# The q and k columns of each attention head as one Strassen pair among the pairs of u and gates

## The chip, the core and the metric

The kernel runs on one core of a Trainium2 chip. The core has five engines with queues of their own: TensorE (PE, matrix products), VectorE (DVE), ScalarE (ACT), GpSimd (POOL) and SyncE (SP, which here only issues transfers). Each works through its queue in order; engines wait for each other by semaphores. On chip are SBUF, from which all engines read, and PSUM, eight banks into which PE writes its sums. The metric is the device time of one execution in microseconds, lower is better; the median of several runs counts.

## What is computed

One layer over 512 tokens of 2048 channels, in float32:

```
h = rms_norm(x)
q | k | v | u | v_sgu | gate_a | gate_b = h @ w_in      # 1024 x5 and 2048 x2 columns
q = rms_norm per head (8 heads of 128) * g_q;  k the same * g_k
z = q k^T / sqrt(128);  beta = sigmoid(z);  keep = sigmoid(-z), s < t only
A[t,s] = beta[t,s] * product of keep[t,j] over s < j < t
y_a = (A v) @ w_oa
y_b = (gelu(u) * (W_s layer_norm(gelu(v_sgu)) + b)) @ w_ob
x = x + (sigmoid(gate_a) * y_a + sigmoid(gate_b) * y_b) @ w_out
x = x + relu(rms_norm(x) @ w_ff1)^2 @ w_ff2               # hidden 8192
```

## The kernel before

Every operand of a large product is held as two parts in a faster matmul format (`hi`, a rounded copy made by ACT, and `lo`, the rest, made by DVE), and a product is three matmuls: hi·hi, hi·lo, lo·hi (`mm3`, lines 70 to 74). A weight piece of 128x1024 is loaded raw, cast by ACT (line 94 or 108) and subtracted by DVE (line 96 or 109) into the pool of pieces `w_piece`, six buffers, so three hi/lo pairs.

Two ways of multiplying stand side by side. `by_token` takes 512 weight columns at a time, holds four PSUM banks (one per 128 tokens) and runs over all 16 row blocks: 192 matmuls of 512 columns. `strassen_pair` takes two blocks of 128 columns and the two halves of the tokens, forms Strassen's seven products (`strassen_columns`, lines 200 to 236; the weight sums on DVE in `Sums.parts`, one of them by an accumulating load that POOL issues, line 183) and leaves the result with channels on the partitions and tokens along the row. Products of one pair and the copies between banks use two of the five banks of `ps_acc`; the three of `ps_aux` hold the forks for the whole run of pairs.

The order of the program around the change: q and k by `by_token` (`heads_of`), v, all twice (four heads each), then v_sgu by `by_token`, then a run of 20 pairs for u and the gates, then y_a and y_b. Beside these products stands a queue of small tasks, `behind`: `step()` takes one from it after each weight piece of `by_token` and after each product of a pair. Through it go the loading of x, the transposes of q and k to channels (`head`), the attention of four heads at once (`attention`: weights, turn, product), the spatial weights and the Strassen factors of h (`gate_factors`, needed before the run of pairs). The final order on each engine is made by a scheduler when the program is built, which starts from the order written and takes what it holds ready first.

For q and k, `heads_of` scales the rows, sums squares per head on POOL and DVE, multiplies by the reciprocal root, and transposes each head's four blocks on PE (line 526). In `weights`, z is `mm3` for each of four token blocks (512, 384, 256, 128 columns), two sigmoids on ACT give beta and keep, DVE does the mask, a running product from the right (line 554) and the multiplication (line 558); `turn` transposes A (line 568) and splits it; `product` multiplies with v and POOL stores the result to memory (`held_o`).

Of the kernel before, what the change touches and what calls it, by code (L numbers as in the profile page):

```python
# [35 lines left out]
def tile_hybrid_layer(ctx: ExitStack, tc: tile.TileContext, x, g_mix, w_in, g_q, g_k, ln_g, ln_b,  # L36
# [426 lines left out]

    load_xk(0)
# [5 lines left out]
    for k in range(CK):  # L470
# [3 lines left out]
    early.extend([weight(w_in[0], CK, 0), (hi, lo)])  # L474
# [3 lines left out]
                   lambda: turn_gains(gains, gT2),  # L478
                   lambda: along(rstd, rstd_b)])
# [7 lines left out]
    scale = float(P) ** -0.5  # L487
# [13 lines left out]
    def heads_of(c0, g0, half, name):  # L501

        n, parts = [], []

        def evac(tb, o):
            raw = slot(name + "_raw")
            nc.scalar.activation(out=raw, in_=o, func=AF.Copy, scale=rstd[:, tb:tb + 1])
            sq = slot("sq")
            nc.gpsimd.tensor_tensor(out=sq, in0=raw, in1=raw, op=ALU.mult)
            m = tiny(4, "m")  # L510
            nc.vector.tensor_reduce(out=m, in_=sq.rearrange("p (h d) -> p h d", d=P), axis=AX.X,
                                    op=ALU.add)
            nc.vector.tensor_scalar(out=m, in0=m, scalar1=1.0 / P, scalar2=EPS, op0=ALU.mult,
                                    op1=ALU.add)
            r = rsqrt(m, 4, "r")
            raw3 = raw.rearrange("p (h d) -> p h d", d=P)
            nc.vector.tensor_tensor(out=raw3, in0=raw3, in1=r.unsqueeze(2).to_broadcast([P, 4, P]),
                                    op=ALU.mult)
            n.append(raw)

        by_token(win, c0 + half * W, hT_at, KT, evac, name)

        def head(h):
            t = aux(name + "T")
            for tb in range(NTB):
                nc.tensor.transpose(out=t[:, tb * P:(tb + 1) * P], in_=n[tb][:, h * P:(h + 1) * P],
                                    identity=ident)
# [6 lines left out]
    def attention(half, qT, kT, v):

        a, aT = {}, {}

        def weights(h):

            room = {0: ("a", 384), 1: ("b", 0), 2: ("a", 0), 3: ("c", 0)}  # L540
            beta = {k: slot("beta") for k in "abc"}
            for tb in (3, 2, 1, 0):
                n = (tb + 1) * P
                key, c = room[tb]
                z = aux("z")
                mm3(z[:, :n], [q[:, tb * P:n] for q in qT[h]], [k[:, :n] for k in kT[h]], True, True)
                b = beta[key][:, c:c + n]
                keep = slot("keep")
                nc.scalar.activation(out=keep[:, :n], in_=z[:, :n], func=AF.Sigmoid, scale=-scale)
                nc.scalar.activation(out=b, in_=z[:, :n], func=AF.Sigmoid, scale=scale)  # L550
                nc.vector.tensor_tensor(out=keep[:, n - P:n], in0=keep[:, n - P:n], in1=later, op=ALU.max)

                rest = slot("rest")
                nc.vector.tensor_tensor_scan(out=rest[:, :n][:, ::-1], data0=keep[:, :n][:, ::-1],
                                             data1=keep[:, :n][:, ::-1], initial=1.0,
                                             op0=ALU.mult, op1=ALU.min)
                nc.gpsimd.tensor_tensor(out=b[:, n - P:], in0=b[:, n - P:], in1=past, op=ALU.mult)
                nc.vector.tensor_tensor(out=b[:, :n - 1], in0=b[:, :n - 1], in1=rest[:, 1:n], op=ALU.mult)
                a[h, tb] = b

        def turn(h):

            hi = {k: slot("aT_hi", F32R) for k in "abc"}
            lo = {k: slot("aT_lo", F32R) for k in "abc"}
            for sb in range(NTB):
                t = aux("aT")
                for tb in range(sb, NTB):
                    nc.tensor.transpose(out=t[:, tb * P:(tb + 1) * P],
                                        in_=a[h, tb][:, sb * P:(sb + 1) * P], identity=ident)
                key, c = {0: ("a", 0), 1: ("b", 0), 2: ("c", 0), 3: ("b", 384)}[sb]  # L570
                n = S - sb * P
                parts = hi[key][:, c:c + n], lo[key][:, c:c + n]
                split_to(*parts, t[:, sb * P:])
                aT[h, sb] = parts

        def product(h):
            o = aux("o")
            for sb in range(NTB):
                mm3(o[:, sb * P:], [p[:, h * P:(h + 1) * P] for p in v[sb]], aT[h, sb],
                    sb == 0, sb == NTB - 1)  # L580
            for i, part in enumerate(split(o, "oT")):
                nc.gpsimd.dma_start(out=held_o[half * 4 + h, i], in_=f32(part))
# [72 lines left out]

# [402 lines left out]
```

## Time and profile before

| | |
|---|---|
| median of three runs | 2428.63 us (2428.33 to 2431.28) |
| profiled execution, its own time | 2426.78 us |
| its span, first to last instruction | 2425.1 us |
| granted PE clock | 1.00 |
| PE, DVE, ACT, POOL busy | 100%, 76%, 49%, 17% |
| q, k, v, v_sgu with attention | 8 to 419 us |
| 20 pairs of u and gates | 419 to 809 us |
| DMA busy share in the pairs | 0.68 |

In the views, a group's row gives the line, engine and operation, output<-inputs, sizes and count, then busy time in all and the mean duration of one, then idle time before it and who ended it. PE's instructions overlap, so that the distance between two starts and not the duration is what one costs. In a timeline row the first number is the start in us, the second the time covered.

### The profile page before, as it was taken

The numbers are of one execution on the slowest core, as the hardware profiler recorded it, in microseconds if no ns is written. First come the engines' busy times: TensorE is split into PE (matmuls) and PEld (weight loads), VectorE is DVE, ScalarE is ACT, GpSimd is POOL, SyncE is SP. The second block draws the span as 40 slices with busy tenths as digits, with TensorE's granted clock in tenths as the row PEclk, the third lists the DMA queues.
The fourth block names the chain that finished last, engine by engine and source line by source line (L and its number), as shares of the span: only waits on it lengthen the run. The fifth ranks groups of instructions, "written<-read, shape, count | busy, mean of one in ns | idle before, by whom it ended". The sixth has DMA issues, their size and how long they took to land.

```text
span 2425.1 us, 34336 instructions
## 1 busy us (share of the span) xinstructions
PE 2414.5 (100%) x12648; PEld 2073.7 (86%) x12648; DVE 1848.1 (76%) x2433; ACT 1199.5 (49%) x1769; POOL 410.3 (17%) x539
## 2 busy tenths in 40 slices
PE   9999999999999999999999999999999999999999
PEld 8888878888888888888988888899888888888887
DVE  4556578777777564444789888888888998989987
ACT  5233344555555322233577776777765443333333
POOL 0203112000011422100001000000024334322210
PEclk9999999999999999999999999999999999999999
DMA  5333234666666944343389888888886999867753
GB/s 183 95 123 104 96 101 151 154 163 165 163 157 159 345 140 148 131 148 124 102 219 238 225 227 233 232 233 223 224 276 247 298 309 320 255 218 209 235 181 97
DMA packets 446169, 463.68 MB, mean 191 GB/s; under 512 B 19568, under 2 KB 330928, under 8 KB 446000
## 3 DMA queue, kind: packets, MB, share of 16 engines
q1 hardware_dynamic: 358352, 332.48, 42.5%
q0 software_dynamic: 87360, 128.48, 23.1%
q8 instruction: 99, 1.62, 0.3%
q10 hardware_dynamic: 288, 0.52, 0.1%
q14 instruction: 70, 0.57, 0.1%
HBM read 374.90 MB, written 85.46 MB: 190 GB/s over the span
## 4 chain that ended last, share of the span: by engine, by line
PE 63%; DVE 0%; ACT 0%; issue 0%; DVEq 0%
PE q L73 9%; PE q L72 9%; PE q L74 9%; PE q L220 7%; PE fork L220 7%; PE fork L223 4%; PE q L223 4%; PE xo L74 2%; PE xo L72 2%; PE xo L73 2%; PE yb L73 1%; PE yb L72 1%; PE yb L74 1%; PE f L73 0%; PE f L74 0%; PE f L72 0%
## 5 line engine op out<-in xcount | busy, mean ns | idle before, releaser
L108 ACT CAST w_hi<-w_raw 128x1024 fp32r<-128x1024 f32 (+1 forms) x583 | 611.9, 1050 | 656.9 <-PE q L73 334.6
L109 DVE TENSOR_TENSOR w_lo<-w_raw,w_hi 128x1024 fp32r<-128x1024 f32 (+1 forms) x583 | 710.7, 1220 | 202.0 <-ACT w_hi L108 192.4
L73 PE MATMUL q<-w_lo,ys 128*128 128x512 f32 x896 | 348.9, 389 | 0.3 <-DVE w_lo L109 0.3
L74 PE MATMUL q<-w_hi,ys 128*128 128x512 f32 x896 | 348.6, 389 | 0.0
L72 PE MATMUL q<-w_hi,ys 128*128 128x512 f32 x896 | 312.6, 389 | 0.7 <-ACT w_hi L108 0.5
L96 DVE TENSOR_TENSOR w_lo<-w_raw,w_hi 128x1024 fp32r<-128x1024 f32 x131 | 164.5, 1255 | 194.1 <-ACT w_hi L94 193.1
L94 ACT CAST w_hi<-w_raw 128x1024 fp32r<-128x1024 f32 x131 | 137.5, 1050 | 316.1 <-issue 81.3
L220 PE MATMUL q<-ys,w_hi 128*128 128x512 f32 x1064 | 271.5, 393 | 0.0
L183 POOL DMA_DIRECT2D w_raw<-in_w_ff_dram x58 | 81.1, 1398 | 900.8 <-ACT act L281 463.1
L220 PE MATMUL fork<-ys,w_hi 128*128 128x512 f32 x904 | 225.9, 391 | 0.0
L220 PEld LDWEIGHTS q<-ys,w_hi 128*128 128x128 f32 x1064 | 189.7, 189 | 31.9
L73 PEld LDWEIGHTS q<-w_lo,ys 128*128 128x128 f32 x896 | 168.2, 188 | 36.4 <-DVE w_lo L109 1.5
L72 PEld LDWEIGHTS q<-w_hi,ys 128*128 128x128 f32 x896 | 168.1, 188 | 36.3 <-ACT w_hi L108 0.9
L74 PEld LDWEIGHTS q<-w_hi,ys 128*128 128x128 f32 x896 | 168.2, 188 | 34.8
L220 PEld LDWEIGHTS fork<-ys,w_hi 128*128 128x128 f32 x904 | 164.5, 189 | 30.8
L957 POOL DMA_DIRECT2D ys<-store x224 | 127.6, 614 | 177.7 <-PE q L74 115.9
L223 PEld LDWEIGHTS q<-ys,w_lo 128*128 128x128 f32 x1064 | 144.8, 190 | 10.6
L223 PE MATMUL q<-ys,w_lo 128*128 128x256 f32 x1064 | 148.0, 282 | 0.0
L1000 DVE SCALAR_TENSOR_TENSOR total<-q,plus,total 128x512 f32<-128x512 f32 x180 | 132.1, 746 | 4.6 <-PE q L74 4.5
L223 PEld LDWEIGHTS fork<-ys,w_lo 128*128 128x128 f32 x904 | 123.3, 190 | 8.8
L223 PE MATMUL fork<-ys,w_lo 128*128 128x256 f32 x904 | 126.1, 282 | 0.0
L74 PE MATMUL q<-ys,w_lo 128*128 128x256 f32 x408 | 115.5, 283 | 0.0
(283 smaller groups left out, 4596.2 us busy)
## 6 DMA issues: line engine op xcount, KB each, us to landing
w_raw<-in_w_ff_dram SPq DMA_DIRECT2D x256, 512.0 KB, 5.6
w_raw<-in_w_in_dram SPq DMA_DIRECT2D x143, 512.0 KB, 4.0
ys<-store POOLq DMA_DIRECT2D x224, 256.0 KB, 6.3
w_raw<-in_w_ff_dram POOLq DMA_DIRECT2D x58, 512.0 KB, 7.3
store<-ys_hi SPq DMA_DIRECT2D x90, 256.0 KB, 4.6
store<-ys_lo SPq DMA_DIRECT2D x90, 256.0 KB, 5.3
w_raw<-in_w_out_dram SPq DMA_DIRECT2D x32, 512.0 KB, 4.2
store<-ys SPq DMA_DIRECT2D x44, 256.0 KB, 5.7
```

Source lines behind the costliest of these rows:

```text
L72: nc.tensor.matmul(o, lhsT=lh[0], rhs=rh[0], start=start, stop=False, **kw)
L73: nc.tensor.matmul(o, lhsT=lh[0], rhs=rh[1], start=False, stop=False, **kw)
L74: nc.tensor.matmul(o, lhsT=lh[1], rhs=rh[0], start=False, stop=stop, **kw)
L94: nc.scalar.copy(out=hi, in_=raw)
L96: nc.vector.tensor_tensor(out=lo, in0=raw, in1=f32(hi), op=ALU.subtract)
L108: nc.scalar.copy(out=hi, in_=src)
L109: state["lo"] = nc.vector.tensor_tensor(out=lo, in0=src, in1=f32(hi), op=ALU.subtract)
L183: state["sum"] = nc.gpsimd.dma_start(out=self.w21, in_=self.blocks[1, 1], accum_op=ALU.add)
L220: nc.tensor.matmul(o, lhsT=hi[:, k, :], rhs=rhs[name][k], start=name == "y11" and k == 0, stop=False, skip_group_check=True)
L223: nc.tensor.matmul(o[:, :HS], lhsT=lo[:, k, :], rhs=rhs[name][k][:, :HS], start=False, stop=k == KH - 1, skip_group_check=True)
L957: nc.gpsimd.dma_start(out=f32(t), in_=store[f][HELD.index(name), p])
L1000: nc.vector.scalar_tensor_tensor(out=a, in0=o, scalar=part, in1=a, op0=ALU.mult, op1=ALU.add)
```

## The change

The 1024 columns of q and of k leave `by_token`. For each head, the 128 columns of q and the 128 of k become the two column blocks of one `strassen_pair`, in the run of u and gates: two gate pairs, then eight times (one head's pair, two gate pairs), then two gate pairs, 28 in all. The result of such a pair is already q and k with channels on the partitions, so that the transposes fall away. What each token's row still needs is its norm: `attend` squares the pair's result on ACT, splits it, sums over the channels with matmuls against a tile of ones (`factors`, four columns wide, output `ms`), and takes the reciprocal root on POOL. The factor of q enters z as the scale of the sigmoids; the factor of k goes along the row by a matmul of ones with diagonal tiles (`scaled_k`, output `rows`) and is multiplied into k with the gains. Attention of one head is 18 tasks, one per product of the pairs after its own. v is now stored in memory by POOL (`held_a`) and fetched for each head; `held_o` is stored by SP in place of POOL. The attention's PSUM tiles come from `ps_acc`, the pool of the products. The factors of h and the spatial weights are made during v and v_sgu.

The diff, cut to its core:

```diff
     def column_sums(wap, c0, loaded=True):
 
         KH = KT // 2
-        blocks = {(h, c): wap[:, c0 + c * P:c0 + (c + 1) * P].rearrange("(k h p) c -> h p k c", p=P, h=2)[h]
+        c0 = c0 if isinstance(c0, tuple) else (c0, c0 + P)
+        blocks = {(h, c): wap[:, c0[c]:c0[c] + P].rearrange("(k h p) c -> h p k c", p=P, h=2)[h]
                   for h in range(2) for c in range(2)}
...
+    gqk = const.tile([P, HEADS], F32, name="gqk")
+    eps_x = const.tile([P, NTB], F32, name="eps_x")
+
+    def head_terms():
+        nc.vector.tensor_tensor(out=gqk, in0=gT2[:, 16:24], in1=gT2[:, 24:32], op=ALU.mult)
+        nc.vector.tensor_scalar(out=gqk, in0=gqk, scalar1=-float(P) ** 0.5, scalar2=0.0, op0=ALU.mult, op1=ALU.add)
+        nc.vector.tensor_scalar(out=eps_x, in0=ms1, scalar1=P * EPS, scalar2=0.0, op0=ALU.mult, op1=ALU.add)
...
+    held_a = dram.tile([2, 2, NTB, P, W], F32, name="held_a")
...
-    def heads_of(c0, g0, half, name):
...
+    def attend(h, act):
+
...
+        def square(src):
+            t = slot("sq")
+            nc.scalar.activation(out=t, in_=src, func=AF.Square)
+            part["sq"] = split(t, "sq")
+
+        def factors():
+            m = acc("ms")
+            for tb in range(NTB):
+                for i, sq in enumerate(part["sq"]):
+                    nc.tensor.matmul(m[:, tb * 4:tb * 4 + 4], lhsT=sq[:, tb * P:(tb + 1) * P], rhs=ones_r[:, :4],
+                                     start=i == 0, stop=i == 1)
+            t, f = small4("ms"), small4("r")
+            nc.vector.tensor_tensor(out=t, in0=m[:, :16].rearrange("p (b r) -> p b r", r=4)[:, :, 0], in1=eps_x,
                                     op=ALU.add)
+            nc.gpsimd.tensor_tensor(out=f, in0=t, in1=mhalf, op=ALU.pow)
+            return f
+
+        def of_q():
+            r[1], r[-1] = factors(), small4("nr")
+            nc.gpsimd.tensor_tensor(out=r[-1], in0=r[1], in1=minus_one, op=ALU.mult)
+            part["q"] = split(q, "qT")
+
+        def of_k():
+            f, f_hi, f_lo = factors(), small4("r_hi", F32R), small4("r_lo")
+            nc.vector.tensor_copy(out=f_hi, in_=f)
+            nc.vector.tensor_tensor(out=f_lo, in0=f, in1=f32(f_hi), op=ALU.subtract)
+            part["dg"] = [slot("dg", F32R) for _ in range(2)]
+            for t, x in zip(part["dg"], (f32(f_hi), f_lo)):
+                for tb in range(NTB):
+                    nc.scalar.activation(out=t[:, tb * P:(tb + 1) * P], in_=ident, func=AF.Copy,
+                                         scale=x[:, tb:tb + 1])
+
+        def scaled_k():
+            rows = acc("rows")
+            for i, t in enumerate(part["dg"]):
+                nc.tensor.matmul(rows, lhsT=ones_r, rhs=t, start=i == 0, stop=i == 1)
+            nc.vector.scalar_tensor_tensor(out=k, in0=k, scalar=gqk[:, h:h + 1], in1=rows, op0=ALU.mult,
+                                           op1=ALU.mult)
+            part["k"] = split(k, "kT")
+
+        def fetch_v():
+            for i in range(2):
+                t = slot("v", F32R)
+                nc.gpsimd.dma_start(out=f32(t).rearrange("p (b c) -> p b c", b=NTB),
+                                    in_=held_a[i, h // 4, :, :, h % 4 * P:(h % 4 + 1) * P].rearrange("b p c -> p b c"))
+                v.append(t)
...
+            z = acc("z")
+            mm3(z[:, :n], [x[:, tb * P:n] for x in part["q"]], [x[:, :n] for x in part["k"]], True, True)
+            b = beta[key][:, c:c + n]
+            nc.scalar.activation(out=keep[:, :n], in_=z[:, :n], func=AF.Sigmoid, scale=r[-1][:, tb:tb + 1])
+            nc.scalar.activation(out=b, in_=z[:, :n], func=AF.Sigmoid, scale=r[1][:, tb:tb + 1])
...
-        steps = [[(weights, 0)], [], [(weights, 1)], [(turn, 0)], [(weights, 2)], [(product, 0), (turn, 1)], [(weights, 3)], [(product, 1), (turn, 2)], [], [(product, 2), (turn, 3)], [], [(product, 3)]]
...
+            for i, x in enumerate(split(o, "oT")):
+                nc.sync.dma_start(out=held_o[h, i], in_=f32(x))
+        return [lambda: square(q), of_q, lambda: square(k), of_k, lambda: None, scaled_k, lambda: None,
+                lambda: weigh(3), lambda: weigh(2), lambda: weigh(1), lambda: weigh(0), fetch_v, lambda: None,
+                lambda: turn(0), lambda: turn(1), lambda: (turn(2), turn(3)), lambda: None, product]
...
-    for half in range(2):
-        qT = heads_of(0, 16, half, "q")
-        kT = heads_of(SBW, 24, half, "k")
-        if half == 0:
-            behind.extend([load_spatial, lambda: None, lambda: spatial(0), lambda: spatial(1)])
-        else:
-            behind.extend([lambda k=k: gate_factors(k) for k in range(4)])
-        v = []
-        by_token(win, 2 * SBW + half * W, hT_at, KT,
-                 lambda tb, o, v=v: v.append(split(o, "v", rstd[:, tb:tb + 1])), "v")
-        if half == 0:
-            behind.extend(attention(half, qT, kT, v))
...
+    VC = 2 * SBW
+    for half in range(2):
+        def evac_h(tb, o):
+            for i, part in enumerate(split(o, "v", rstd[:, tb:tb + 1])):
+                nc.gpsimd.dma_start(out=held_a[i, half, tb], in_=f32(part))
+
+        if half:
+            steps = collections.defaultdict(list)
+            base = len(behind)
+            steps[0].append(load_spatial)
+            steps[2].append(lambda: spatial(0))
+            steps[4].append(lambda: spatial(1))
+            for k in range(KT // 2):
+                steps[3 + 2 * k].append(lambda k=k: gate_factors(k))
+            for k in range(KT):
+                steps[10 + k // 4].append(lambda k=k: moved(k))
+            room = []
+            steps[16 - base].append(lambda: room.extend(slot("vg") for _ in range(NTB)))
+            at_steps(steps)
+        by_token(win, VC + half * W, hT_at, KT, evac_h, "v")
...
+    order = gate_pairs[:2]
+    for h in range(HEADS):
+        order += [h] + gate_pairs[2 * h + 2:2 * h + 4]
+    order += gate_pairs[2 * HEADS + 2:]
...
+        if isinstance(item, int):
+            behind.extend(attend(item, strassen_pair(win, (item * P, SBW + item * P), hy, forks)))
+        else:
+            c0, n, func = item
+            gated(n, strassen_pair(win, c0, hy, forks, ready=opened.pop() if opened else None), func)
```

How the built program differs, at three places. On PE, four transposes of a head of q stood between k's products:

```order
L72 MATMUL k<-w_hi,hT 128x512
L73 MATMUL k<-w_lo,hT 128x512
L74 MATMUL k<-w_hi,hT 128x512
L526 MATMUL qT<-ident,q_raw 128x128 x4
L72 MATMUL k<-w_hi,hT_both 128x512
L73 MATMUL k<-w_lo,hT_both 128x512
L74 MATMUL k<-w_hi,hT_both 128x512
L72 MATMUL k<-w_hi,hT_both 128x512
```

Now the sums of squares of q stand among the products of the following gate pair (`q` and `fork` are the pair's banks, `sq` the squares, `ones_r` the ones):

```order
L224 MATMUL q<-ys,w_lo 128x256 x6
L532 MATMUL ms<-ones_r,sq_hi 128x4
L224 MATMUL q<-ys,w_lo 128x256 x2
L221 MATMUL fork<-hT,w_hi 128x512 x6
L532 MATMUL ms<-ones_r,sq_lo 128x4
L532 MATMUL ms<-ones_r,sq_hi 128x4
L532 MATMUL ms<-ones_r,sq_lo 128x4
L532 MATMUL ms<-ones_r,sq_hi 128x4
L532 MATMUL ms<-ones_r,sq_lo 128x4
L532 MATMUL ms<-ones_r,sq_hi 128x4
L532 MATMUL ms<-ones_r,sq_lo 128x4
L221 MATMUL fork<-hT,w_hi 128x512 x2
```

The transposes are gone, and eight narrow matmuls that wait for DVE's `sq_lo` stand between the products of the pair. On DVE, the weights of a head stood almost without weight pieces between them, in the stage of the projections:

```order
L554 SCALAR_TENSOR_TENSOR rest<-keep 128x512
L551 TENSOR_TENSOR keep<-keep,later 128x128
L558 TENSOR_TENSOR beta<-beta,rest 128x511
L554 SCALAR_TENSOR_TENSOR rest<-keep 128x384
L558 TENSOR_TENSOR beta<-beta,rest 128x383
L551 TENSOR_TENSOR keep<-keep,later 128x128
L554 SCALAR_TENSOR_TENSOR rest<-keep 128x256
L558 TENSOR_TENSOR beta<-beta,rest 128x255
L96 TENSOR_TENSOR w_lo<-w_raw,w_hi 128x1024
L551 TENSOR_TENSOR keep<-keep,later 128x128
L554 SCALAR_TENSOR_TENSOR rest<-keep 128x128
L558 TENSOR_TENSOR beta<-beta,rest 128x127
```

Now they stand among the weight pieces (line 109) and weight sums (lines 181, 185) of a gate pair:

```order
L581 TENSOR_TENSOR keep<-keep,later 128x128
L584 SCALAR_TENSOR_TENSOR rest<-keep 128x512
L588 TENSOR_TENSOR beta<-beta,rest 128x511
L109 TENSOR_TENSOR w_lo<-w_raw,w_hi 128x1024
L581 TENSOR_TENSOR keep<-keep,later 128x128
L181 TENSOR_TENSOR w_raw<-w_raw 128x1024
L584 SCALAR_TENSOR_TENSOR rest<-keep 128x384
L109 TENSOR_TENSOR w_lo<-w_raw,w_hi 128x1024
L581 TENSOR_TENSOR keep<-keep,later 128x128
L588 TENSOR_TENSOR beta<-beta,rest 128x383
L109 TENSOR_TENSOR w_lo<-w_raw,w_hi 128x1024
L185 TENSOR_TENSOR w_raw<-w_raw 128x1024
```

Each block's running product (line 584) is followed by a weight piece that a later product of the pair needs. On POOL's queue, the accumulating loads of the run of pairs (line 183) followed each other up to the fetches of the attention's result:

```order
L686 DMA held_v<-vg 128x512 x4
L699 TENSOR_TENSOR rv<-ve,mhalf 128x4
L183 DMA w_raw<-in_w_in_dram 128x8x128 x19
L491 DMA oT<-held_o 128x512 x13
L491 DMA gate<-held_g 128x512 x4
```

Now a head's reciprocal roots, the mask on beta and the fetch of v stand between them:

```order
L724 TENSOR_TENSOR rv<-ve,mhalf 128x4
L183 DMA w_raw<-in_w_in_dram 128x8x128 x4
L537 TENSOR_TENSOR r<-ms,mhalf 128x4 x2
L542 TENSOR_TENSOR nr<-r,minus_one 128x4
L587 TENSOR_TENSOR beta<-beta,past 128x128 x3
L183 DMA w_raw<-in_w_in_dram 128x8x128
L587 TENSOR_TENSOR beta<-beta,past 128x128
L566 DMA v<-held_a 128x4x128 x2
L183 DMA w_raw<-in_w_in_dram 128x8x128 x2
L537 TENSOR_TENSOR r<-ms,mhalf 128x4 x2
```

The accumulating load of a gate pair is issued after three of a head's four `beta` multiplications.

More of the change, by code (lines that the diff above doesn't have):

```diff
@@ L362, in tile_hybrid_layer @@
     nc.gpsimd.memset(mhalf, -0.5)
+    minus_one = const.tile([P, 4], F32, name="minus_one")
+    nc.gpsimd.memset(minus_one, -1.0)
+    ones_r = const.tile([P, P], F32R, name="ones_r")
+    nc.vector.tensor_copy(out=ones_r, in_=ones)
     def rsqrt(ms, n, name):
@@ L534, in attention @@
[L534 to L564, printed above, removed]
-            for sb in range(NTB):
[L566 to L582, printed above, removed]
-        steps = [[(weights, 0)], [], [(weights, 1)], [(turn, 0)], [(weights, 2)], [(product, 0), (turn, 1)], [(weights, 3)], [(product, 1), (turn, 2)], [], [(product, 2), (turn, 3)], [], [(product, 3)]]
-        return [lambda fs=fs: [f(h) for f, h in fs] for fs in steps]
@@ new lines, in attend, with small4, weigh, turn @@
+    def attend(h, act):
+        q, k = act
+        part, r, v, a = {}, {}, [], {}
+        beta, hi, lo, aT = {}, {}, {}, {}
+        def small4(name, dt=F32):
+            return small.tile([P, NTB], dt, name=name, tag=name, bufs=3)
+        def square(src):
[10 more added lines that the diff above has]
+            nc.vector.tensor_tensor(out=t, in0=m[:, :16].rearrange("p (b r) -> p b r", r=4)[:, :, 0], in1=eps_x,
+                                    op=ALU.add)
+            nc.gpsimd.tensor_tensor(out=f, in0=t, in1=mhalf, op=ALU.pow)
[26 more added lines that the diff above has]
+                v.append(t)
+        def weigh(tb):
+            key, c = {0: ("a", 384), 1: ("b", 0), 2: ("a", 0), 3: ("c", 0)}[tb]
+            if not beta:
+                beta.update({x: slot("beta") for x in "abc"})
+            n = (tb + 1) * P
+            z = acc("z")
+            mm3(z[:, :n], [x[:, tb * P:n] for x in part["q"]], [x[:, :n] for x in part["k"]], True, True)
+            b = beta[key][:, c:c + n]
+            keep = slot("keep")
+            nc.scalar.activation(out=keep[:, :n], in_=z[:, :n], func=AF.Sigmoid, scale=r[-1][:, tb:tb + 1])
+            nc.scalar.activation(out=b, in_=z[:, :n], func=AF.Sigmoid, scale=r[1][:, tb:tb + 1])
+            nc.vector.tensor_tensor(out=keep[:, n - P:n], in0=keep[:, n - P:n], in1=later, op=ALU.max)
+            rest = slot("rest")
+            nc.vector.tensor_tensor_scan(out=rest[:, :n][:, ::-1], data0=keep[:, :n][:, ::-1],
+                                         data1=keep[:, :n][:, ::-1], initial=1.0,
+                                         op0=ALU.mult, op1=ALU.min)
+            nc.gpsimd.tensor_tensor(out=b[:, n - P:], in0=b[:, n - P:], in1=past, op=ALU.mult)
+            nc.vector.tensor_tensor(out=b[:, :n - 1], in0=b[:, :n - 1], in1=rest[:, 1:n], op=ALU.mult)
+            a[tb] = b
+        def turn(sb):
+            if not hi:
+                hi.update({x: slot("aT_hi", F32R) for x in "abc"})
+                lo.update({x: slot("aT_lo", F32R) for x in "abc"})
+            t = acc("aT")
+            for tb in range(sb, NTB):
+                nc.tensor.transpose(out=t[:, tb * P:(tb + 1) * P], in_=a[tb][:, sb * P:(sb + 1) * P],
+                                    identity=ident)
+            key, c = {0: ("a", 0), 1: ("b", 0), 2: ("c", 0), 3: ("b", 384)}[sb]
+            n = S - sb * P
+            aT[sb] = hi[key][:, c:c + n], lo[key][:, c:c + n]
+            split_to(*aT[sb], t[:, sb * P:])
+        def product():
+            o = acc("o")
+            for sb in range(NTB):
+                mm3(o[:, sb * P:], [x[:, sb * P:(sb + 1) * P] for x in v], aT[sb], sb == 0, sb == NTB - 1)
+            for i, x in enumerate(split(o, "oT")):
[3 more added lines that the diff above has]
+                lambda: turn(0), lambda: turn(1), lambda: (turn(2), turn(3)), lambda: None, product]
@@ L714, in fetch_o @@
         oT.append([fetched(held_o[h, i], "oT", F32R, pool) for i in range(2)])
[L716 to L717 removed]
+    for i, item in enumerate(order):
+        if i == len(order) - 1:
             with tc.issue_after(state["sum"].ins):
```

49 lines of the change are left out of this document (5 added, 44 removed).

## The prediction

> **What bounds the kernel now.** I read the page first, then the waits of TensorE (PE), then the busy time by stretch.
>
> ```profile
> span 2425.1 us, 34336 instructions
> PE 2414.5 (100%) x12648; PEld 2073.7 (86%) x12648; DVE 1848.1 (76%) x2433; ACT 1199.5 (49%) x1769; POOL 410.3 (17%) x539
> PE 63%; DVE 0%; ACT 0%; issue 0%; DVEq 0%
> ```
>
> PE is busy for all of the span but 10.6 us, and the chain of waits never leaves it for long. The waits of PE, in full, say how little stands between its instructions:
>
> ```profile
> PE vg L72 <- DVE v_lo L112: 2.4, 1, 2.4
> PE ya L72 <- DVE merged_a L792: 1.6, 2, 1.3
> PE idle L351 <- POOL ones L347: 1.2, 1, 1.2
> PE q L72 <- ACT w_hi L108: 0.5, 1, 0.5
> PE q L73 <- DVE w_lo L109: 0.3, 1, 0.3
> PE q L72 <- DVE total L1000: 0.2, 1, 0.2
> PE o L72 <- DVE aT_lo L109: 0.2, 1, 0.2
> ```
>
> So the time is the length of PE's stream, and the change has to be priced as instructions of PE taken out and put in, plus new waits. The other engines count where they can no longer keep ahead of PE. By stretch (projections and attention; the 20 Strassen pairs of u and gates; most of the pairs of w_ff1):
>
> ```profile
> core 0: us, PE busy (x) PEld busy (x) DVE busy (x) ACT busy (x) POOL busy (x), PEclk, DMA share, GB/s
> 8.00:418.70 410.70, 407.96 (x1948) 338.39 (x1947) 258.32 (x439) 170.31 (x312) 73.26 (x88) 1.00 0.37 119
> 418.70:808.90 390.20, 390.20 (x2388) 350.44 (x2388) 303.77 (x360) 219.43 (x319) 42.16 (x43) 1.00 0.68 171
> 1210.00:1780.00 570.00, 570.00 (x3487) 511.86 (x3486) 499.37 (x699) 406.33 (x641) 47.84 (x34) 1.00 0.88 230
> ```
>
> The clock is full (1.00) throughout. VectorE (DVE) is at 63%, 78% and 88%, and in the last stretch PE still has no gap: that is what DVE can carry here without being felt.
>
> **The change, PE's stream first.** A matmul's own duration (389 ns) overlaps the next, so I price by distance between starts.
>
> ```profile
> 302.07 0.39 PE L72 MATMUL v<-w_hi,hT 128*128 128x512 f32 x1
> ...
> 308.19 0.39 PE L72 MATMUL vg<-w_hi,hT 128*128 128x512 f32 x1
> ```
>
> 27 matmuls apart, 6.12 us: 227 ns for 512 columns; beside attention some starts lie 234 ns apart, so I take 228.
>
> ```profile
> 422.20 0.28 PE L72 MATMUL q<-ys,w_hi 128*128 128x256 f32 x1
> ...
> 794.85 0.28 PE L72 MATMUL q<-ys,w_hi 128*128 128x256 f32 x1
> ```
>
> These are the first matmul of the m7 product in the first and the last of 20 pairs, 19 pairs apart: 372.65/19 = 19.61 us a pair.
>
> ```profile
> L72 PE MATMUL k<-w_hi,hT 128*128 128x512 f32 x104 | 41.1, 398 | 0.0
> L72 PE MATMUL k<-w_hi,hT_both 128*128 128x512 f32 x24 | 9.6, 399 | 0.0
> L526 PE MATMUL kT<-ident,k_raw 128*128 128x128 f32 x32 | 5.4, 271 | 0.0
> ```
>
> Removed: k has 128 matmuls in each of the lines 72, 73 and 74, q as many: 768 x 0.228 = **175.1 us out**. Added: 8 pairs x 19.61 = **156.9 us in**. Also out are 32 transposes each for k and q, whose pace the transposes of aT show:
>
> ```profile
> 178.65 0.39 PE L72 MATMUL q<-w_hi,hT_both 128*128 128x512 f32 x1
> 178.88 0.92 PE L568 MATMUL aT<-ident,beta 128*128 128x128 f32 x7
> 179.56 0.48 PE L73 MATMUL q<-w_lo,hT_both 128*128 128x512 f32 x1
> 179.88 0.40 PE L74 MATMUL q<-w_hi,hT_both 128*128 128x512 f32 x1
> ```
>
> From 178.65 to 179.88 is 1.23 us; two 512-column matmuls take 0.46 of it, so seven transposes take 0.77, 0.110 us each. 64 x 0.110 = **7.0 us out**.
>
> In their place come, for each head, two `rows` matmuls of 512 columns: 16 x 0.228 = **3.6 us in**; and 16 small `ms` matmuls (the sums of squares: 4 columns wide, each with 128x128 new weights), 128 in all. No such shape stands in the trace. The nearest row is z of the last block, 128 columns wide:
>
> ```profile
> 165.28 0.39 PE L74 MATMUL q<-w_hi,hT 128*128 128x512 f32 x1
> 165.50 0.22 PE L72 MATMUL z<-kT_hi,qT_hi 128*128 128x128 f32 x1
> 165.56 0.28 PE L73 MATMUL z<-kT_lo,qT_hi 128*128 128x128 f32 x1
> 165.68 0.27 PE L74 MATMUL z<-kT_hi,qT_lo 128*128 128x128 f32 x1
> 165.79 0.44 PE L72 MATMUL q<-w_hi,hT 128*128 128x512 f32 x1
> 166.07 0.40 PE L73 MATMUL q<-w_lo,hT 128*128 128x512 f32 x1
> ```
>
> From 165.28 to 166.07 is 0.79 us, less two wide matmuls 0.33: 0.11 us for each of three, as for the transposes, which have other data and one pass. What they share is the weight load, so a narrower matmul should cost the same: 128 x 0.11 = **14.3 us in** (0.112 unrounded). The low end is the 0.06 us between the first two of them (the load already done): 128 x 0.058 = 7.4. The high end is a wide matmul, 0.228 each, 29.2; I keep 0.112, as two unlike shapes agree on it.
>
> The Trainium skill, page "TensorE: Matmul & The Clock Gate", section "LDWEIGHTS (loading the stationary operand)", has the load at columns/1.2 ns, so 107 ns for 128 columns: the trace agrees with 110. The Trainium skill's same page (section "Wait — 56ns, not 53.3ns?") lets starts come down to about 25 ns however narrow the matmul; if that floor held with new weights each time, the 128 would take an estimated 3.2 us.
>
> Sum of the stream: -175.1 + 156.9 - 7.0 + 3.6 + 14.3 = **-7.3 us**. The attention's z, aT and o are the same instructions in another place and cost the same.
>
> **What could make PE wait.** First the load. What attention costs DVE, from the grouped rows of eight heads:
>
> ```profile
> L554 DVE TENSOR_TENSOR_SCAN rest<-keep 128x512 f32<-128x512 f32 (+3 forms) x32 | 27.0, 842 | 0.7
> L558 DVE TENSOR_TENSOR beta<-beta,rest 128x511 f32<-128x511 f32 (+3 forms) x32 | 17.5, 546 | 2.1
> L109 DVE TENSOR_TENSOR aT_lo<-aT,aT_hi 128x512 fp32r<-128x512 f32 (+3 forms) x32 | 14.9, 486 | 6.2 <-ACT aT_hi L108 6.2
> L551 DVE TENSOR_TENSOR keep<-keep,later 128x128 f32<-128x128 f32 x32 | 12.3, 385 | 5.4 <-ACT keep L549 5.4
> L109 DVE TENSOR_TENSOR oT_lo<-o,oT_hi 128x512 fp32r<-128x512 f32 x8 | 5.5, 686 | 0.4 <-ACT oT_hi L108 0.4
> L112 DVE SCALAR_TENSOR_TENSOR kT_lo<-kT,gT,kT_hi 128x512 fp32r<-128x512 f32 x8 | 5.8, 746 | 2.6 <-ACT kT_hi L111 2.6
> ```
>
> The first five are 77.2/8 = 9.7 us a head. New per head are four `lo` parts of 512 columns (sq twice, q, k: 0.69 each), one three-operand scaling (0.75): 3.5; the four-column ones are left out. A pair costs DVE 303.77/20 = 15.2. A head's three pairs then are 45.6 + 9.7 + 3.5 = 58.8 us of DVE. PE has 58.8 of pairs, z and o at 1.9 each (three matmuls of each of four widths at 228 ns per 512 columns, the narrowest 0.11), ten aT 1.1, ms 1.8 and rows 0.5: 66.0. DVE is at 89%; high by the two gate multiplications that a head's own pair lacks. In the pairs of w_ff1 88% costs PE nothing, so on average DVE keeps up. ACT has 219.43/20 = 11.0 us a pair, half of the head's 66 us, and its 27 attention instructions fit into the other half at up to 1.2 us each. The DMA engines get 1 MB more a head, 16 GB/s on 171, and ran at 230 in w_ff1. The stage ahead of the pairs shrinks to 410.7 - 175.1 = 236 us and keeps at most 258.32 - 77.2 = 181 us of DVE's work, 77%.
>
> The tight place is weigh(3) to turn(3), about six products: DVE has 6/7 x 15.2 = 13.0 plus (27.0 + 17.5 + 14.9 + 12.3)/8 = 9.0, so 22.0 us, against 6/7 x 19.61 = 16.8 + z 1.9 + aT 1.1 = 19.8 on PE. DVE falls 2.2 us behind. Its cover is the weight pieces made ahead: six buffers are three hi/lo pairs, one in use and two ahead, up to two products or 5.6 us. So I cost the backlog at nothing; without that cover it is 2.2 us a head.
>
> Next the waits that the tasks add to PE's own queue: ms waits for sq_lo, rows for the diagonals, z for kT_lo, o for aT_lo; behind each in the queue stand the pair's next products. In stage one the same kind of wait (z, aT, o) cost PE 0.2 us in eight heads. I take 0.15 a head, 1.2, with ends at 0 and at the largest wait seen, 2.4 a head. The evacuation of v now frees its banks only after ACT and DVE, as at the one v-to-vg change that cost 2.4; there are still two such changes, and I add 0.6.
>
> The queues: the two held_o stores go from POOL to SP, ahead of six weight loads of the next pair, which wait with them if oT is late; these loads serve products a pair later (19.6 us). On POOL the accumulating load of a gate pair now stands behind three `beta` multiplications, yet its sum is needed three products later. ACT gets two more table loads (five in the order, three before; the order of gelu pairs and a sigmoid head), at the row's
>
> ```profile
> L704 ACT ACT_TABLE_LOAD x1 | 1.3, 1283 | 0.0
> ```
>
> 2.6 us of an engine with a third of its time free. All of these I cost at nothing; each would cost its lateness, once a head.
>
> Total -7.3 + 1.2 + 0.6 = **-5.5 us**. The profiled execution took 2426.78 (its span 2425.1), so 2421.3 there; the median of the three runs is 1.85 above it, 2428.63, so **2423.1** as the timed median, 0.23% less.
>
> **Rivals.**
> - *Small waits eat the gain.* With 0.3 to 1.5 us a head at ms, rows or z, 2.4 to 12 us go back in place of 1.2: 2424.3 to 2434. For it: each head repeats the same order, so one lateness is paid eight times, and the engines that PE waits for are fuller than in stage one. Against: the 0.2 us above.
> - *DVE's backlog is not covered (slower).* If the pieces ahead are only one product, or DVE must stand at `keep` until z is done and so starts the stretch with nothing ahead, its lag is paid in each head. It decides from 1.5 us a head (12 + 0.6 - 7.3 = +5.3). At 2.2, and at 4.0 with one block's keep, scan and multiplication on top (0.39 + 0.84 + 0.55 = 1.8), it gives 17.6 to 32 + 0.6 - 7.3: 2440 to 2454. Against: between the first z and the first weight piece that DVE makes after its `keep`, the order leaves PE a third of m7, three z and two and a half products, about 2.8 x 2.8 + 1.2 = 9 us, and DVE's block takes 1.8 of it.
> - *The ms matmuls cost less.* At 0.058 the sum is 6.9 us lower, 2416. By the 25 ns floor of the Trainium skill's page "TensorE: Matmul & The Clock Gate" it would be an estimated 2412.
> - *The pair is no cheaper among attention.* If starts of the 28 pairs stretch from 228 to 236 ns, 28 x 48 x 0.008 = 10.8 us are lost: +5.3, 2434. Against: the pairs of w_ff1 keep the pace with more DVE and DMA.
>
> **How the numbers follow.** Forecast 0.48 (own range 2421 to 2426, of which 0.38 lies below the bound), small waits 0.27, backlog 0.12, cheaper ms 0.08, stretched pairs 0.05. About 0.2% (4.9 us) is what a measurement here can tell from no change, so under 2423.8 is faster: 0.38 + 0.08 + 0.04 of the small waits = 0.50. Slower needs over 2433.5: the backlog and a little of the stretched pairs, 0.13. Same 0.37. The range 2415 to 2434 leaves out most of the backlog case and the lowest ms price.
>
> **What would show it.** Right: the first m7 of neighbouring pairs stays 19.6 us apart apart from the heads' own matmuls (about 66 us for three pairs); groups of eight ms take 0.9 us; PE's waits in the pairs sum to under 3 us; the run of ya starts about 5.5 us earlier. Wrong: waits of PE on sq_lo, kT_lo or w_lo that repeat every 66 us; DVE without idle time for a whole head; ms at 0.06 us.

## The result

The changed kernel takes 2515.03 us (median of four runs, 2513.32 to 2515.92), the kernel before 2429.76: a ratio of 1.035, 95% interval 1.0332 to 1.0368. It is **3.5% slower**, 85 us, where 2423.1 was forecast and 2434 was the upper end of the range.

The page of the changed kernel, its first lines and the engines of the chain of waits:

```profile
span 2513.4 us, 35343 instructions
PE 2460.3 (98%) x12920; PEld 2090.3 (83%) x12920; DVE 1908.5 (76%) x2541; ACT 1278.4 (51%) x1931; POOL 434.5 (17%) x556
PE 61%; DVE 1%; DMA 0%; issue 0%; ACT 0%; ACTq 0%; DVEq 0%
```

PE now stands for 53 us of the span (10.6 before), and it is also *busy* 46 us longer, which more waits can't explain. The first is told by the waits of PE, in full again down to 0.5 us:

```profile
PE aT L597 <- DVE beta L588: 32.6, 8, 5.2
PE q L221 <- ACT fork L229: 11.3, 8, 1.4
PE ya L72 <- DVE merged_a L825: 1.6, 2, 1.3
PE idle L352 <- POOL ones L348: 1.2, 1, 1.2
PE xT L437 <- DVE hT L112: 1.0, 1, 1.0
PE q L73 <- DVE w_lo L109: 0.7, 2, 0.5
PE q L72 <- ACT w_hi L108: 0.5, 1, 0.5
```

Eight waits, one a head, of the aT transposes for DVE's last beta, and eight for the copy of a fork by ACT. The same place in the second head, from PE's timeline, then DVE's:

```profile
366.08 0.39 PE L74 MATMUL z<-kT_hi,qT_lo 128*128 128x512 f32 x1
...
377.95 1.11 PE L224 MATMUL fork<-hT,w_lo 128*128 128x256 f32 x8
382.98 1.11 PE L597 MATMUL aT<-ident,beta 128*128 128x128 f32 x4 [3.91 <-DVE beta L588]
```

```profile
367.28 0.29 DVE L581 TENSOR_TENSOR keep<-keep,later 128x128 f32<-128x128 f32 x1 [2.77 <-ACT keep L579]
367.60 1.22 DVE L584 TENSOR_TENSOR_SCAN rest<-keep 128x512 f32<-128x512 f32 x1
...
381.50 1.22 DVE L109 TENSOR_TENSOR w_lo<-w_raw,w_hi 128x1024 fp32r<-128x1024 f32 x1
382.64 0.28 DVE L588 TENSOR_TENSOR beta<-beta,rest 128x127 f32<-128x127 f32 x1
```

DVE stands 2.77 us at its first `keep`, because it is next in its queue and z, from which ACT makes `keep`, is not there; then it runs from 367.28 to 382.92, 15.6 us, and the last thing it makes is what PE wants. PE has 12.6 us of matmuls there, from the end of z (366.47) to 379.07. The first head waits 1.3 us longer (5.2), because ACT there loads a table between the end of z (290.33) and its first sigmoid:

```profile
290.40 1.28 ACT L579 ACT_TABLE_LOAD   x1 [2.28 <-issue]
```

Part of the longer busy time is the clock. By stretch, the wait of that head, and a time soon after it:

```profile
core 0: us, PE busy (x) PEld busy (x) DVE busy (x) ACT busy (x) POOL busy (x), PEclk, DMA share, GB/s
379.00:383.00 4.00, 0.09 (x2) 0.03 (x1) 4.00 (x9) 0.51 (x2) 0.00 (x0) 0.93 1.09 300
383.70:385.60 1.90, 1.90 (x7) 1.51 (x6) 1.90 (x4) 0.59 (x1) 0.00 (x0) 0.50 0.14 36
```

The granted clock falls to 0.50 about when the wait ends, from 0.9 us before to 1.1 us after. In the trace's record of the granted clock there are eight such times, one at each wait at aT, five of 3.4 us and three of 6.8; the falls lie 75.1 or 71.7 us apart, 22 or 21 steps of 3.41 us. The Trainium skill, page "TensorE: Matmul & The Clock Gate", section "HAM oscillation — how this bites in real kernels", has PE keep its clock if it does not idle longer than about 3.4 us. The waits here, 3.9 to 5.2 us, agree with it, but shorter ones can do it too: in e1 below, PE's one wait of 2.4 us, for v's evacuation ahead of vg, is followed by 3.4 us at 0.50.

```profile
316.85 0.50 PE L72 MATMUL vg<-w_hi,hT 128*128 128x512 f32 x1 [2.42 <-DVE v_lo L112]
317.30:320.60 3.30, 3.30 (x10) 2.53 (x9) 3.27 (x6) 2.73 (x7) 1.52 (x3) 0.50 0.00 0
```

The same wait of 2.4 us in the profiled execution of the kernel before left the clock at 1.00. Here the measurement decides: no limit at 3.4 us shows.

The rest is in no wait and at a clock of 1.00. y_b's product has the same instructions in the same order in both kernels; its hi·hi rows give count, shortest, median and longest duration, and the first and last start, before and after:

```profile
L72 PE MATMUL yb<-sT_hi,w_hi x128: 389/389/389, 908.7 to 995.0; 128*128 128x512 f32 x128
```

```profile
L72 PE MATMUL yb<-sT_hi,w_hi x128: 395/396/396, 969.4 to 1058.3; 128*128 128x512 f32 x128
```

Every third matmul of 512 columns is one of these, so 127 x 3 = 381 starts took 86.3 us before, 226.5 ns each, and 88.9 after, **233.3 ns**. The same shows from v (228 to 233) to w_ff2 (226.8 to 233.3), also where nothing was changed and PE waits for nobody.

### The profile page after: what moved, and what is told of

It reads as the page before. It is cut to its first block, busy times and chain, and to the rows that moved or that the text cites. A ratio compares the mean times of both kernels' runs of the same rounds, so it can differ in the third digit from the quotient of the medians.

```text
span 2513.4 us, 35343 instructions
## 1 busy us (share of the span) xinstructions
PE 2460.3 (98%) x12920; PEld 2090.3 (83%) x12920; DVE 1908.5 (76%) x2541; ACT 1278.4 (51%) x1931; POOL 434.5 (17%) x556
## 4 chain that ended last, share of the span: by engine, by line
PE 61%; DVE 1%; DMA 0%; issue 0%; ACT 0%; ACTq 0%; DVEq 0%
PE q L72 9%; PE q L73 9%; PE q L74 9%; PE fork L221 7%; PE q L221 7%; PE fork L224 4%; PE q L224 4%; PE xo L74 2%; PE xo L72 2%; PE xo L73 2%; PE yb L73 1%; PE yb L74 1%; PE yb L72 1%; DMA store<-ys 0%; PE f L72 0%; PE f L73 0%
## 5 line engine op out<-in xcount | busy, mean ns | idle before, releaser
L108 ACT CAST w_hi<-w_raw 128x1024 fp32r<-128x1024 f32 (+1 forms) x639 | 669.3, 1048 | 719.8 <-PE q L73 338.4
L109 DVE TENSOR_TENSOR w_lo<-w_raw,w_hi 128x1024 fp32r<-128x1024 f32 (+1 forms) x639 | 780.3, 1222 | 245.9 <-ACT w_hi L108 230.2
L221 PE MATMUL q<-ys,w_hi 128*128 128x512 f32 x1192 | 311.1, 398 | 11.3 <-ACT fork L229 11.3
L221 PEld LDWEIGHTS q<-ys,w_hi 128*128 128x128 f32 x1192 | 210.5, 188 | 50.3 <-ACT fork L229 13.0
L221 PE MATMUL fork<-ys,w_hi 128*128 128x512 f32 x968 | 245.6, 395 | 0.0
L96 DVE TENSOR_TENSOR w_lo<-w_raw,w_hi 128x1024 fp32r<-128x1024 f32 x99 | 124.7, 1259 | 144.4 <-ACT w_hi L94 144.2
L94 ACT CAST w_hi<-w_raw 128x1024 fp32r<-128x1024 f32 x99 | 103.7, 1048 | 238.7 <-issue 84.5
L224 PEld LDWEIGHTS q<-ys,w_lo 128*128 128x128 f32 x1192 | 162.5, 188 | 13.4
L224 PE MATMUL q<-ys,w_lo 128*128 128x256 f32 x1192 | 165.8, 281 | 0.0
L72 PE MATMUL q<-ys,w_hi 128*128 128x256 f32 x472 | 133.2, 282 | 0.0
```

What stands on the lines that cost most here:

```text
L72: nc.tensor.matmul(o, lhsT=lh[0], rhs=rh[0], start=start, stop=False, **kw)
L94: nc.scalar.copy(out=hi, in_=raw)
L96: nc.vector.tensor_tensor(out=lo, in0=raw, in1=f32(hi), op=ALU.subtract)
L108: nc.scalar.copy(out=hi, in_=src)
L109: state["lo"] = nc.vector.tensor_tensor(out=lo, in0=src, in1=f32(hi), op=ALU.subtract)
L221: nc.tensor.matmul(o, lhsT=hi[:, k, :], rhs=rhs[name][k], start=name == "y11" and k == 0, stop=False, skip_group_check=True)
```

## The experiments

**What slows the matmuls.** The change adds some small tiles (`minus_one`, `ones_r`, `gqk`, `eps_x`, and five names in `small`). As the built programs lay SBUF out, they move the weight pieces from byte 22528 to 23136 of a partition, and the slots, which hold the other operand, from 47360 to 48448. (The traces hold no addresses; the shifts follow from the tiles' sizes. The constants lie ahead of the pieces and move both; `small` lies between the two and moves the slots alone.) Before, pieces and slots both lay on multiples of 256. e1 moves both by 32 bytes, e2 the pieces alone; the tiles are never written, so no instruction is added and each engine's order stays.

```diff
 e1     nc.gpsimd.memset(mhalf, -0.5)
+       pad = const.tile([P, 4], F32, name="pad")
 e2     nc.gpsimd.memset(mhalf, -0.5)
+       pad = const.tile([P, 8], F32, name="pad")
+       gap = small.tile([P, 56], F32, name="gap", tag="gap", bufs=1)
```

> The kernel before with one unwritten tile of 16 bytes a partition among the constants, so that every weight piece and every slot lies 32 bytes higher (before: the pieces at 22528 and up, a multiple of 256; now 22560); the order on every engine is the one of before. In the changed kernel the pieces lie at 23136, which is 32 above a multiple of 64, and 512-column matmuls start 233 ns apart instead of 227 even in stages that the change leaves alone (w_ff1 and w_ff2, 1266.1 us instead of 1245.4, +1.66%). Theory A (the place of the operands in SBUF sets the pace): 233 ns here too, and a time of 2430 + 1.66% = about 2470 us. Theory B (the pace comes from something else in the changed kernel, such as its order or its load): 227 ns and 2428 to 2432 us.

> The kernel before with only the weight pieces moved up by 32 bytes (22560); a second unwritten tile of 224 bytes puts the slots and raw tiles back on multiples of 256. Theory A with the pieces as the cause: 233 ns and about 2470 us, as with everything moved. Theory A with the slots as the cause: 227 ns and 2430 us. Theory B: 2430 us.

e1: 2429.53 us, ratio 1.0002 (0.9992 to 1.0011). e2: 2465.22, ratio **1.0148** (1.0133 to 1.0164). The rows of y_b in e1, then e2:

```profile
L72 PE MATMUL yb<-sT_hi,w_hi x128: 389/389/389, 910.7 to 997.0; 128*128 128x512 f32 x128
```

```profile
L72 PE MATMUL yb<-sT_hi,w_hi x128: 395/396/396, 921.1 to 1010.0; 128*128 128x512 f32 x128
```

So both forms of theory A, as written, were half right: neither the place of the pieces nor that of the slots counts, for e1 moved both to no effect. What counts is the **distance between the two operands of a product**. It was 24832 bytes before and in e1, a multiple of 256; 25312 after, and 25056 in e2, both 224 modulo 256. So of the new tiles only the five in `small` count, 15 buffers of 32 bytes. The raw tiles, which ACT and DVE read beside the pieces, moved with the slots in every run. But in y_b the starts between which DVE, ACT and POOL all stood idle (59 in the changed kernel, 54 before) lie 233.4 and 226.7 ns apart, as the others do, so the reading of those engines is not what slows PE.

e3 gives the changed kernel its distance back, with nothing else touched:

```diff
+       pad = const.tile([P, 40], F32, name="pad")
+       gap = small.tile([P, 8], F32, name="gap", tag="gap", bufs=1)
```

> The changed kernel with two unwritten tiles (160 and 32 bytes), so that pieces and slots lie on multiples of 256 again, as before; its order is unchanged. Theory A: 227 ns in w_ff1 and w_ff2 and about 1.66% less of 2515, so 2470 to 2476 us; the eight waits at aT (32.6 us) and at the fork (11.3 us) stay. Theory B: 233 ns and 2515 us.

2480.73 us, ratio 1.021 (1.0193 to 1.0227): 34.3 us less than the changed kernel, a little less than the 39 to 45 expected, since the pairs hardly gain from it (668.2 us instead of 669.4 with attention). The waits stay, as expected:

```profile
PE aT L597 <- DVE beta L588: 33.0, 8, 5.2
PE q L221 <- ACT fork L229: 11.6, 8, 1.7
```

e8 asked how far the rule reaches, with the slots of the kernel before 64 bytes further on:

```diff
+       gap = small.tile([P, 16], F32, name="gap", tag="gap", bufs=1)
```

> The kernel before with the slots and raw tiles moved up by 64 bytes and the pieces left where they were. Moving everything by 32 cost nothing (2429.5), moving the pieces alone by 32 cost 36 us (2465.2): so it is the distance between the two operands, not the place of either. If it counts only within 64 bytes, a distance of 64 costs nothing: 227 ns and 2428 to 2432 us. If any distance off a multiple of 128 or 256 costs: 233 ns and about 2465 us.

2440.99 us, ratio 1.0052 (1.0038 to 1.0066): neither of the two answers. The stages differ in sign. Lengths from first to last start of a stage (xo: 768 matmuls with the piece as the moving operand; w_ff1: 32 Strassen pairs with the piece as the weights; w_ff2: moving again). The 627.8 and 616.9 us in the expectation of e9 leave the last two products of w_ff1 out:

| slots minus pieces, modulo 256 | xo, us | w_ff1, us | w_ff2, us |
|---|---|---|---|
| 0 (before) | 179.8 | 633.4 | 611.6 |
| 224 (e2) | 184.1 | 636.4 | 628.3 |
| 64 (e8) | 184.3 | 622.4 | 628.1 |

At 64 the pairs are *faster* than at 0 (512 columns every 228.7 ns instead of 230.1, 256 columns every 115.4 instead of 119.3), xo and w_ff2 as slow as at 224. The piece's role alone doesn't decide it: in y_b the pieces are the weights too, and its hi·hi rows take 86.3 us at 0, 87.2 at 64 and 88.9 at 224.

**What the waits come from, and what they cost.** e4 leaves the addresses of the changed kernel and puts two empty tasks ahead of turn(0):

```diff
-                lambda: weigh(3), lambda: weigh(2), lambda: weigh(1), lambda: weigh(0), fetch_v, lambda: None,
+                lambda: weigh(3), lambda: weigh(2), lambda: weigh(1), lambda: weigh(0), fetch_v, lambda: None, lambda: None, lambda: None,
```

> The changed kernel with two more empty tasks between weigh(0) and turn(0), so that the aT transposes come two products (5.6 us) later. Theory C (PE waits because DVE's last beta is about 4 us late, and the wait halves the clock for 3.4 to 6.8 us after it): the 32.6 us of waits at aT go, and with them most of the half clock (37.5 us at half speed, about 19 us): 2515 - 33 - 15 to 19 = 2463 to 2467 us. Rival (DVE is short of time for the whole head, so the lateness moves on to the weight pieces): the waits turn up at w_lo or a later aT, with the same sum, and the time stays within 10 us of 2515.

2452.36 us, ratio 1.0096 (1.008 to 1.0111): 62.7 us less, more than the 48 to 52 expected. The clock is 1.00 throughout, and of the waits there is left:

```profile
PE ya L72 <- DVE merged_a L825: 1.6, 2, 1.3
PE q L221 <- ACT fork L229: 1.4, 1, 1.4
```

The rival, that the lateness would move on to the pieces, is out. The surplus is the fork: in the changed kernel the scheduler had put m6 directly behind y11 once in each head, and m6 must wait until ACT has copied y11's sum away; with the later turn, another product (sixteen `fork<-hT`) stands between them in seven of eight heads. That is read from the two orders; no run moved m6 alone.

e6 and e7 keep PE's order as it was (on multiples of 256, as e3) and take work from DVE instead: e6 leaves out the mask of the diagonal, e7 the running product:

```diff
 e6 -            nc.vector.tensor_tensor(out=keep[:, n - P:n], in0=keep[:, n - P:n], in1=later, op=ALU.max)
 e7 -            rest = slot("rest")
    -            nc.vector.tensor_tensor_scan(out=rest[:, :n][:, ::-1], data0=keep[:, :n][:, ::-1],
    -                                         data1=keep[:, :n][:, ::-1], initial=1.0,
    -                                         op0=ALU.mult, op1=ALU.min)
    +            rest = keep
```

> The changed kernel on multiples of 256 (2480.7 us) without DVE's four operations keep<-keep,later a head; the mask of the diagonal is left out of the weights, PE's order stays as it was. DVE runs from its first keep to the last beta for 15.6 us without a pause, PE has 12.6 us of matmuls there. Theory D (DVE's own work in this stretch is what PE waits for): the four operations are 4 x 0.385 = 1.5 us, so each wait at aT falls from 3.96 to 2.4 us (the first from 5.2 to 3.7), 12.3 us in all: 2468 us if the half clock stays, down to 2448 if waits of 2.4 us no longer bring it. Rival (the lateness comes from ACT's sigmoid or from z, and DVE only follows): the waits stay at 3.9 us and the time at 2478 to 2483.

> The same kernel as the base, without DVE's four scans a head (the multiplication reads keep in place of rest; the running product is left out of the weights), PE's order unchanged. Theory D: 4 x 0.842 = 3.4 us less of DVE, the waits at aT fall to about 0.6 us (the first to 1.8), 33.0 to 6 us in all, and the clock stays full: 2480.7 - 27 - 20.5 (41 us at half clock) = 2433 us; the waits at the fork (11.6 us) stay. If short waits bring the half clock too: 2454 us. Rival: no change of the waits, 2478 to 2483.

e6: 2442.44 us, ratio 1.0056 (1.0042 to 1.0069). e7: 2430.76, ratio 1.0007 (0.9998 to 1.0016). Waits of e6, then e7:

```profile
PE q L221 <- ACT fork L229: 11.6, 8, 1.7
PE aT L597 <- DVE beta L588: 8.5, 8, 2.2
```

```profile
PE q L221 <- ACT fork L229: 11.6, 8, 1.7
...
PE aT L597 <- DVE beta L588: 0.2, 1, 0.2
```

Theory D holds: less work on DVE, shorter waits, and with these waits, of 2.2 us and less, the clock stays at 1.00. In e6 the waits fell by 3.1 us a head and not by 1.5, because DVE's order changed too: two of the five `w_lo` (1.2 us each) and one addition of an evacuation that stood ahead of the last beta now stand behind it (in e7 too).

The price of the half clock follows from PE's busy time, with the same instructions and addresses, in e3 and in e5 (below):

```profile
PE 2424.6 (98%) x12920; PEld 2094.0 (84%) x12920; DVE 1906.0 (77%) x2541; ACT 1279.3 (52%) x1931; POOL 437.9 (18%) x556
```

```profile
PE 2407.0 (100%) x12920; PEld 2081.4 (86%) x12920; DVE 1904.7 (79%) x2541; ACT 1280.2 (53%) x1931; POOL 438.5 (18%) x556
```

17.6 us, or 16.1 against e7's 2408.5, which has PE's order of e3 too: about 2 us for each wait, on top of the wait. The changed kernel against e4, on the addresses of both, gives 19.3 (2460.3 less 2441.1).

**Both mended.** e5 is e3 and e4 together:

> Both edits together: turn(0) two products later, and pieces and slots on multiples of 256. If the place of the operands and the waits are separate causes, their gains add: 2515.0 - 62.7 (as the later turn alone gave) - 34.3 (as the place alone gave) = 2418.0 us, 2415 to 2421, and faster than the kernel before (2429). That would also be the sum that the prediction made for PE's stream, near its 2423.1. If they overlap (the place costs only where PE is late anyway, or the other way round), 2425 to 2452.

2418.62 us (2417.7 to 2420.09), ratio **0.9958** (0.9944 to 0.9972): faster than the kernel before, and 0.6 from the sum of the two gains. So they are separate causes. e10 puts turn(0) one product later instead of two (one empty task):

> The changed kernel on multiples of 256 with turn(0) one product later instead of two. In the order PE then has, between the last z of 512 columns and the first aT, matmuls for 14.9 us in the first head and 17.1 us in the others (12.2 in the changed kernel, 17.6 and 19.8 with two products); DVE's last beta ends 16.5 us after z. So one wait of about 1.5 us is left in the first head and none in the others, the clock stays full, and the time is 2418 to 2422 us. If DVE's lateness grows with the room it is given (pieces put ahead of the last beta), waits of 1 us or more stay in every head: 2427 or more.

2420.38 us, ratio 0.9967 (0.9953 to 0.998), one wait at aT:

```profile
PE aT L597 <- DVE beta L588: 1.3, 1, 1.3
```

One product is enough: the order's matmuls between z and aT, against DVE's 16.5 us, told the waits beforehand, head by head.

Then the distance once more. e9 adds to e5 a view that begins 64 bytes into the tile, for the pieces of the Strassen pairs alone:

```diff
-        return wpool.tile([P, CK * W], F32R, name=name, tag="w_piece", bufs=6)
+        return wpool.tile([P, CK * W + 32], F32R, name=name, tag="w_piece", bufs=6)[:, at:at + CK * W]
...
+            at = 16 if src.shape[1] == KT // 2 else 0; hi, lo = piece("w_hi", at), piece("w_lo", at)
```

> The version with the later turn (2418.6 us), with the weight pieces of the Strassen pairs alone read and written 64 bytes further on in their tiles; all other pieces keep a distance of 128 bytes (modulo 256) to the slots. With the slots 64 bytes off, the kernel before was faster where the pieces are the weights: 20 pairs of u and gates 389.5 to 384.7 us, the 32 of w_ff1 627.8 to 616.9, and slower where the pieces are the moving operand. If that holds for the pieces of these pairs alone: 28 pairs save 6.7, w_ff1 10.9, so 2401 us; and if a distance of 128 is as good as 0 or 256, the products by token (xo, w_ff2) keep 227 ns. If 128 costs too, those take up to 2.8% more of some 985 us (stage one, xo, w_ff2): up to 2428.

2426.08 us, ratio 0.9988 (0.9979 to 0.9997), a miss, and the expectation misstated its own layout: a piece then takes 4224 bytes, 16.5 times 256, so that from one buffer to the next the distance alternates between 128 and 0, and between 64 and 192 for the pairs. The starts of w_ff2 spread from 226 to 236 ns, mean 230.6; what 128 alone costs, no run shows. e11 gives pieces 4352 bytes, 17 times 256, and pays with one of the 64 slots:

```diff
-SLOTS = 64
+SLOTS = 63
...
+        return wpool.tile([P, CK * W + 64], F32R, name=name, tag="w_piece", bufs=6)[:, at:at + CK * W]
...
+            at = 0 if src.shape[1] == KT // 2 else 16; hi, lo = piece("w_hi", at), piece("w_lo", at)
```

> The later turn (2418.6 us) with both distances at once: the slots lie 64 bytes (modulo 256) above the pieces of the Strassen pairs and 0 above all others. To make room, pieces take 4352 bytes and there are 63 slots instead of 64. The run before this one had 128 for the others, which cost 230.5 ns instead of 227. If the distance between a product's two operands alone sets its pace: stage one, xo and w_ff2 at 227 ns as with 0, the pairs at 228.8 and 115 to 116.5 ns as with 64 in the kernel before, so 2418.6 - 6.7 - 10.9 = 2401 us, 2398 to 2406. If the missing slot makes something wait, that shows in PE's waits; if the gain of the pairs depends on the place and not the distance, 2416 to 2424.

2402.89 us (2401.18 to 2403.44), ratio **0.9895** (0.9878 to 0.9911), the best version: xo 179.7, w_ff1 623.1, w_ff2 612.6 us, so each of these stages is within 1 us of its better distance, and the missing slot makes nothing wait:

```profile
span 2400.9 us, 35269 instructions
PE 2389.9 (100%) x12920; PEld 2067.2 (86%) x12920; DVE 1904.4 (79%) x2541; ACT 1277.3 (53%) x1931; POOL 439.4 (18%) x556
PE ya L72 <- DVE merged_a L825: 1.7, 2, 1.3
PE q L221 <- ACT fork L229: 1.4, 1, 1.4
```

## Why the prediction was wrong

The sum of the pieces, from the mended version back to the changed kernel: 2418.6 + 34.3 (distance of the operands) + 32.6 (aT) + 9.9 (fork, 11.3 less the one wait that e5 keeps) + about 17 (half clock) = 2512, against 2515.0 measured; with the 19.3 of e4 it is 2515. Step by step:

- **PE's stream, -7.3 us: right.** With both causes mended, PE is busy 2407.0 us instead of 2414.5, so -7.5, and the span is 7.2 shorter (2417.9, before 2425.1) where -5.5 in all was forecast. The price of the new ms matmuls held:

```profile
269.80 0.25 PE L532 MATMUL ms<-ones_r,sq_hi 128*128 128x4 f32 x1
...
270.36 0.25 PE L532 MATMUL ms<-ones_r,sq_lo 128*128 128x4 f32 x1
270.47 2.11 PE L221 MATMUL q<-ys,w_hi 128*128 128x512 f32 x8
```

Six in 0.67 us, 0.112 each. That rules out the cheaper ms. It also rules out, as their price, the 25 ns floor of the Trainium skill's page "TensorE: Matmul & The Clock Gate" (section "Wait — 56ns, not 53.3ns?"). A head with its three pairs takes, by the same z matmul in the third and the last head of e5,

```profile
414.25 0.40 PE L74 MATMUL z<-kT_hi,qT_lo 128*128 128x512 f32 x1
...
744.48 0.40 PE L74 MATMUL z<-kT_hi,qT_lo 128*128 128x512 f32 x1
```

330.23/5 = 66.05 us, where the prediction's sum was 66.0. In the changed kernel it was 74.0.
- **The small waits, 1.2: right in size, not in place. v's evacuation, 0.6: wrong in sign.** e5 has 1.4 at a fork and 1.3 at w_lo in all, none at ms, rows, z or o; the 2.4 us at vg are gone instead of 0.6 more.
- **The backlog of DVE, "costed at nothing": wrong, 4.1 us a head.** The step that failed is its cover, "the weight pieces made ahead", up to 5.6 us. Pieces made ahead cover a product whose piece is late. They don't cover the last beta, which DVE makes in its turn behind five pieces, and which aT, at a fixed place in PE's queue, needs itself. The rival on the backlog had the mechanism, DVE standing at `keep`, and with 4.0 us a head nearly the right price. That it came so near is partly luck: it added one block's 1.8 us to a lag of 2.2, where the runs show 16.4 us of DVE less 12.6 of PE. And the argument against it, 9 us of PE's work between the first z and the first piece after it, asked about the piece and not about the beta. The question to ask of the order was: PE's work between z and aT, 12.2 us (12.6 measured), against the 15.6 + 0.8 us DVE needs from z to the last beta. A table load of ACT, costed at nothing as well, added 1.3 us in the first head.
- **What a wait brings after it: left out, 16 to 19 us.** The rival's 2440 to 2454 took each wait at its length. Full clock before the change was no ground for full clock after it.
- **The fork: not seen, 9.9 us.** The prediction took the order within a pair as unchanged. The order of the built program shows the change and could have been read.
- **The operands' places: not seen, 34.3 us.** The new small tiles were priced at nothing, like everything without an instruction. This term alone would have made the change slower: 2423.1 + 34.3 is 2457.
- **Stretched pairs, priced for the pairs only.** Starts did stretch to 233, but in the whole kernel, and attention beside them wasn't the reason: at distance 0 (e5) the pairs' 512-column starts are 230.2 ns apart (starts over 260 ns left out), 230.1 before.

## What to carry to other kernels

For work that one engine hands to another at a fixed place in the queue, add up both engines' work between hand-over and hand-back in the order as built; spare stock of something else that the late engine makes doesn't count as cover. Each wait of 3.9 us and more here brought a half clock of about 2 us behind it, and some of 2.3 to 2.4 us did too, so such waits are to be priced with it. And a change that adds even small tiles between the operands of a product should be compared with its addresses put back before it is judged: here that was worth 34 us, some five times the gain that was sought, while a tile ahead of both (e1) cost nothing.

## What the runs showed of the hardware

- The distance between the addresses of a matmul's two operands sets its pace, at full clock. For 512 columns with the piece as the moving operand: 226.8 ns at a multiple of 256 bytes, 233.3 at 224, 233.3 at 64. With the piece as the weights, in Strassen pairs: 512 and 256 columns every 230.1 and 119.3 ns at 0, 233.2 and 118.7 at 224, 228.7 and 115.4 at 64. With the piece as the weights in y_b, 512 columns: 226.5, 233.3 and 228.9. Shifting both operands by 32 bytes changes nothing. That the reading of the next weights collides with the reading of the moving operand would fit; no run shows it, and the other distances weren't tried singly.
- The clock fell to 0.50 at every wait of 3.9 us and more, and after one of 2.4 (e1) and one of 2.3 (e2, e8), for 3.4 or 6.8 us; it stayed at 1.00 with a wait of 2.4 in the kernel before, and with waits of 2.2 and less. So length alone does not decide; that the falls lie on a grid of 3.41 us steps would fit a check at fixed times, which no run tested.
